# Output gate tiles of a hybrid attention layer: products of 256 moving columns instead of 512

## The chip, the cores and the metric

The kernel runs on one core of a Trainium2 chip. The metric is the device time of one execution, in microseconds (us). The time before is the median of three runs, 2978.56 us.

## What is computed

One decoder layer over 512 tokens of width 2048, in float32. After a norm and a conditioning shift, `h` is projected by `w_in`; one branch is windowed attention, the other a gated delta rule with 32 heads of 128 channels; both are gated, merged and projected back. The part that the change touches is `dz`, the gate of the delta branch's heads:

```
proj = h @ w_in
aq, ak, av, ag, d_qkv, dz, db, da, mg_a, mg_b = split(proj)
...
o = gated_delta_rule(dq, dk, dv, g, beta)
o = rms_norm(o, dn_norm_w) * silu(dz.reshape(B, T, 32, 128))
y_b = o.reshape(B, T, 4096) @ w_o_dn
```

## The kernel before, in words

All large products are made as channel tiles: 128 output channels on the partitions, the 512 tokens as moving columns, one PSUM tile `mm` of 128 x 512. The contraction over 2048 channels goes in 16 steps of 128 (`kt`). Every float32 operand is kept as two reduced-precision parts, `hh` and `hl` for the activations, `whi` and `wlo` for the weights, and a step is three products in `mm3`: `whi` with `hh` (L240), `whi` with `hl` (L241), `wlo` with `hh` (L242). So a tile is 48 products, and each product is recorded with a weight load (PEld) of its own.

Weights come as 1 MB tiles `raw` in a fixed list of jobs (`plan`). They are split in halves of 1024 columns, eight `kt` steps each: ScalarE casts `whi` (L61), VectorE subtracts for `wlo` (L62). Three buffers hold halves. `half` takes the next one, `half_done` frees it and puts the split of a later half and the next load on a list of due work.

The order around the products is set by `pump`. Every second `kt` step, so eight times a tile, `channel_tile` calls it: it starts due splits and loads, and moves each live generator by a step. Generators are the small work of the heads: convolutions, transposes (L274), the products of the scan (L841 to L901), evictions. So passes of other kinds stand between products of a tile. Inside one engine a scheduler then settles the order of what the program issued.

In the stage of the heads (`delta_heads`, `heads`) each of 16 groups makes five tiles: one of queries, two of values, two of gates. The gate tiles are read by `zgate`: ScalarE takes a scaled copy `zh` (L764) and a tanh (L766) from PSUM, VectorE joins them (L768). Two PSUM buffers `mm` take turns.

Names in the rows: `oh` and `ol` are the split activations of a later projection, `po` and `pv` products of the scan, `pto` and `xtp` transposes, `pu`, `py` and `tt` parts of the scan's preparation.

Of the kernel before, what the change touches and what calls it, by code (L numbers as in the profile page):

```python
# [7 lines left out]
F32 = mybir.dt.float32  # L8
# [8 lines left out]
P = 128  # L17
T = 512
D = 2048
KT = D // P  # L20
# [25 lines left out]
class Layer:  # L46
# [197 lines left out]
    def channel_tile(self, name, xh=None, xl=None):  # L244

        xh, xl = (self.hh, self.hl) if xh is None else (xh, xl)
        ps = self.pmm.tile([P, T], F32, tag="mm", name="mm")
        for kt in range(KT):
            if kt % 8 == 0:
                hi, lo = self.half(name)  # L250
            s = slice((kt % 8) * P, (kt % 8) * P + P)
            self.mm3(ps, (hi[:, s], lo[:, s]), (xh[:, kt, :], xl[:, kt, :]), kt == 0, kt == KT - 1)
            if kt % 2:
                self.pump()
            if kt % 8 == 7:
                self.half_done()
        return ps

    def merge_gate(self, name, j, dst):
# [492 lines left out]
    def heads(self, wk, g):  # L752

        st = {"z": []}
        self.go(self.queries(wk, g, self.channel_tile(f"q{g}"), st), 0)
        for e in range(2):
            self.go(self.values(wk, g, e, self.channel_tile(f"v{2 * g + e}"), st), 0)
        for e in range(2):
            self.go(self.zgate(wk, self.channel_tile(f"z{2 * g + e}"), st), 0)

    def zgate(self, wk, ps, st):
        nc = self.nc
# [753 lines left out]
```

## Time and profile before

| | |
|---|---|
| timed runs | 2980.03, 2968.28, 2978.56 us |
| profiled execution | 2967.88 us, span 2966.1 us |
| granted TensorE clock, mean | 0.991 |
| busy: TensorE, weight loads | 2876.7 us, 2355.9 us |
| busy: VectorE, ScalarE, GpSimd | 1775.4, 1089.9, 201.8 us |
| HBM read, written | 415.26 MB, 78.33 MB |

One execution is profiled. Busy time is what an engine's records cover; matmuls overlap, so the start of one product to the start of the next is the pace, not a record's length. A row of the timeline has start, length, engine, line, operation, output and inputs, shapes (weights 128*128, moving 128x512), and in brackets the idle time ahead of it with what ended it. A granted clock of 1.0 is full speed, 0.5 half.

### The profile page before, as it was taken

Reading aid. Unit: us, or ns where it says so; the run is one execution under the profiler, and the core shown is the slowest. Engines: PE = TensorE matmul, PEld = TensorE weight load, DVE = VectorE, ACT = ScalarE, POOL = GpSimd, SP = SyncE. Lnnn points to the kernel's source line nnn. Section 1 sums busy time; section 2 is a strip of 40 time slices with the busy share of each in tenths; the row PEclk is TensorE's granted clock in tenths of the full one; section 3 lists DMA queues with packets and bytes.
Section 4 is the critical chain, followed back from the end, with each engine's and each line's share of the span. In section 5 each row is a group of like instructions: output and inputs, shape, how many; then the busy total and the mean of one; then the engine's idle time right before and its main releaser. Section 6 shows DMA issues by size and latency. Waiting matters only on the chain.

```text
span 2966.1 us, 38006 instructions
## 1 busy us (share of the span) xinstructions
PE 2876.7 (97%) x14524; PEld 2355.9 (79%) x14524; DVE 1775.4 (60%) x2903; ACT 1089.9 (37%) x2103; POOL 201.8 (7%) x188
## 2 busy tenths in 40 slices
PE   6899999999999999999999999999999999999999
PEld 5677777877878778888888888888887887888887
DVE  5766899699865544545454444454545555434666
ACT  3355333333543433333333333333333232222343
POOL 0012220010000000001100000000100000000000
PEclk8999999999999999999999999999999999999999
DMA  9855645632332233333333333334338998855684
GB/s 334 315 161 188 180 134 163 171 96 75 103 116 88 89 132 124 116 122 127 115 124 125 108 122 108 122 115 125 105 114 304 317 320 293 296 169 176 233 325 173
DMA packets 184871, 498.31 MB, mean 168 GB/s; under 512 B 75217, under 2 KB 77777, under 8 KB 147313
## 3 DMA queue, kind: packets, MB, share of 16 engines
q1 hardware_dynamic: 184690, 495.90, 50.1%
q8 instruction: 114, 1.87, 0.3%
q14 instruction: 67, 0.55, 0.1%
HBM read 415.26 MB, written 78.33 MB: 166 GB/s over the span
## 4 chain that ended last, share of the span: by engine, by line
PE 78%; DVE 11%; DMA 6%; ACT 2%; issue 2%; SPq 0%; POOL 0%; DVEq 0%; POOLq 0%; ACTq 0%
PE mm L240 21%; PE mm L241 20%; PE mm L242 20%; DVE wlo L62 2%; PE m L242 2%; PE m L241 2%; PE m L240 2%; DMA oraw<-o_d 2%; DVE A L735 2%; DVE atmp L729 2%; DVE wa L403 1%; DMA E<-g_rows 1%; DMA gw<-in_w_ada_gate 1%; PE po L901 1%; PE pv L882 1%
## 5 line engine op out<-in xcount | busy, mean ns | idle before, releaser
L240 PE MATMUL mm<-hh,whi 128*128 128x512 f32 x2784 | 1134.4, 407 | 3.6 <-ACT mth L263 3.6
L242 PE MATMUL mm<-hh,wlo 128*128 128x512 f32 x2784 | 1093.3, 393 | 0.0
L241 PE MATMUL mm<-hl,whi 128*128 128x512 f32 x2784 | 1091.0, 392 | 0.0
L62 DVE TENSOR_TENSOR wlo<-raw,whi 128x1024 fp32r<-128x1024 f32 (+1 forms) x484 | 590.2, 1221 | 483.7 <-ACT whi L61 460.5
L61 ACT CAST whi<-raw 128x1024 fp32r<-128x1024 f32 (+1 forms) x484 | 504.8, 1044 | 938.6 <-PE mm L241 829.9
L242 PEld LDWEIGHTS mm<-hh,wlo 128*128 128x128 f32 x2784 | 524.8, 189 | 114.2 <-issue 0.7
L240 PEld LDWEIGHTS mm<-hh,whi 128*128 128x128 f32 x2784 | 525.9, 189 | 112.5 <-issue 8.3
L241 PEld LDWEIGHTS mm<-hl,whi 128*128 128x128 f32 x2784 | 526.4, 189 | 99.6 <-issue 0.8
L240 PE MATMUL mm<-oh,whi 128*128 128x512 f32 x512 | 202.5, 397 | 6.9 <-ACT oh L61 6.9
L241 PE MATMUL mm<-ol,whi 128*128 128x512 f32 x512 | 201.6, 394 | 0.6 <-DVE ol L62 0.6
L242 PE MATMUL mm<-oh,wlo 128*128 128x512 f32 x512 | 201.0, 393 | 0.0
L240 PEld LDWEIGHTS mm<-oh,whi 128*128 128x128 f32 x512 | 97.0, 190 | 29.5 <-ACT oh L61 8.6
L241 PEld LDWEIGHTS mm<-ol,whi 128*128 128x128 f32 x512 | 97.2, 190 | 23.0 <-DVE ol L62 2.1
L242 PEld LDWEIGHTS mm<-oh,wlo 128*128 128x128 f32 x512 | 97.3, 190 | 20.4
L735 DVE TENSOR_TENSOR A<-A,atmp 128x62 f32<-128x62 f32 (+30 forms) x124 | 110.8, 894 | 2.0
L729 DVE TENSOR_TENSOR atmp<-A 128x62 f32<-128x62 f32 (+30 forms) x124 | 109.5, 883 | 1.6
L829 POOL TENSOR_TENSOR qe<-qe,yq 128x512 f32<-128x512 f32 x32 | 46.7, 1479 | 921.9 <-DMA qe<-eg_rows 921.9
L698 POOL TENSOR_TENSOR E<-E,neg_g 128x512 f32<-128x512 f32 x64 | 75.0, 1173 | 412.2 <-DMA E<-g_rows 356.9
L875 DVE SCALAR_TENSOR_TENSOR r<-pp,neg_eg,vt 128x128 f32<-128x128 f32 x96 | 29.3, 346 | 92.4 <-PE pp L872 90.5
L1220 ACT ACTIVATE sm<-sm,mx,rs 128x256 f32<-128x256 f32 (+1 forms) x128 | 71.8, 562 | 5.0 <-DVE mx L1215 5.0
L566 DVE SCALAR_TENSOR_TENSOR yv<-mm,convh,yv 128x511 f32<-128x511 f32 (+2 forms) x96 | 71.4, 744 | 1.7
L403 DVE SCALAR_TENSOR_TENSOR wa<-wa,silu_cb 128x2048 f32<-128x2048 f32 x24 | 54.8, 2283 | 6.5 <-DMA silu_cb<-silu_d 6.5
(337 smaller groups left out, 3025.9 us busy)
## 6 DMA issues: line engine op xcount, KB each, us to landing
raw<-in_w_ch SPq DMA_DIRECT2D x158, 1024.0 KB
wa<-in_w_ada_ss SPq DMA_DIRECT2D x32, 1024.0 KB
raw<-in_w_od SPq DMA_DIRECT2D x32, 1024.0 KB
E<-g_rows SPq DMA_DIRECT2D x64, 256.0 KB
q<-in_w_out SPq DMA_DIRECT2D x32, 512.0 KB
gw<-in_w_ada_gate SPq DMA_DIRECT2D x16, 1024.0 KB
f_d<-q SPq DMA_DIRECT2D x32, 512.0 KB
raw<-in_w_os SPq DMA_DIRECT2D x16, 1024.0 KB
```

Source lines behind the costliest of these rows:

```text
L61: self.nc.scalar.copy(out=hi, in_=src)
L62: self.nc.vector.tensor_tensor(out=lo, in0=src, in1=hi.bitcast(F32), op=ALU.subtract)
L240: nc.tensor.matmul(ps, lhsT=wh, rhs=xh, start=first, stop=False)
L241: nc.tensor.matmul(ps, lhsT=wh, rhs=xl, start=False, stop=False)
L242: nc.tensor.matmul(ps, lhsT=wl, rhs=xh, start=False, stop=last)
L403: nc.vector.scalar_tensor_tensor(out=wa, in0=wa, scalar=1.0, in1=scb, op0=ALU.mult, op1=ALU.mult, accum_out=t[:, j : j + 1])
L566: nc.vector.scalar_tensor_tensor(out=y[:, s:], in0=ps[:, : T - s], scalar=w[:, j : j + 1], in1=y[:, s:], op0=ALU.mult, op1=ALU.add)
L698: nc.gpsimd.tensor_tensor(out=E, in0=E, in1=ng, op=ALU.add)
L729: eng.tensor_tensor(out=t, in0=A[:, m : m + 1, m + 1 :].to_broadcast([P, m, n]), in1=A[:, :m, m : m + 1].to_broadcast([P, m, n]), op=ALU.mult,
L735: eng.tensor_tensor(out=A[:, :m, m + 1 :], in0=A[:, :m, m + 1 :], in1=t, op=ALU.add)
L829: nc.gpsimd.tensor_tensor(out=qf, in0=qf, in1=q, op=ALU.mult)
L1220: nc.scalar.activation(t, t, AF.Exp, scale=r[:, h : h + 1], bias=mx[:, h : h + 1], accum_out=den[:, h : h + 1])
```

## The change

The gate tiles are made by a new function, `gate_tile`, in place of `channel_tile`. It takes the same two weight halves in the same order. Within a half it goes over the tokens in two halves of 256, and for each over the eight `kt` steps, so that each weight tile of 128 x 128 is used twice, first for tokens 0 to 255 and then for 256 to 511, in products of 256 moving columns. The start flag stands on the tile's first product alone, the stop flag on its last. `pump` is called after every fourth step of 256 columns, which is eight times a tile as before, and `half_done` after a half's last product.

```diff
+    def gate_tile(self, name):
+
+        ps = self.pmm.tile([P, T], F32, tag="mm", name="mm")
+        for k in range(2):
+            hi, lo = self.half(name)
+            for t in range(2):
+                ts = slice(t * 256, (t + 1) * 256)
+                for j in range(8):
+                    s, kt = slice(j * P, (j + 1) * P), 8 * k + j
+                    x = (self.hh[:, kt, ts], self.hl[:, kt, ts])
+                    self.mm3(ps[:, ts], (hi[:, s], lo[:, s]), x, kt == 0 and t == 0, kt == KT - 1 and t == 1)
+                    if j % 4 == 3:
+                        self.pump()
+            self.half_done()
+        return ps
...
         for e in range(2):
-            self.go(self.zgate(wk, self.channel_tile(f"z{2 * g + e}"), st), 0)
+            self.go(self.zgate(wk, self.gate_tile(f"z{2 * g + e}"), st), 0)
```

On TensorE, the order of the program before, where the last product of a value tile and a pass of the scan (`pqk`) are followed by the first gate tile:

```order
L242 MATMUL mm<-hh,wlo 128x512
L833 MATMUL pqk<-yq,kT 128x128 x4
L240 MATMUL mm<-hh,whi 128x512
L241 MATMUL mm<-hl,whi 128x512
L242 MATMUL mm<-hh,wlo 128x512
```

The same place of the program now:

```order
L242 MATMUL mm<-hh,wlo 128x512
L849 MATMUL pqk<-yq,kT 128x128 x4
L240 MATMUL mm<-hh,whi 128x256
L241 MATMUL mm<-hl,whi 128x256
L242 MATMUL mm<-hh,wlo 128x256
```

From there to the end of the second gate tile 192 products of 256 columns stand where there were 96 of 512. The same passes stand between them: `py` after 24, `pu` after 48, then `ptv`, `pv`, `pd` with `po`, and `pp`.

On VectorE, before, where the first gate tile of a group passes into its second half (`yv` is a convolution of the values, `tt` the solved matrix that the scan takes, `zh` a gate, `vs` an operand of the scan):

```order
L573 SCALAR_TENSOR_TENSOR yv<-th,yv 128x512
L62 TENSOR_TENSOR wlo<-raw,whi 128x1024
L850 TENSOR_TENSOR tt_9047<-pu,neg_beta 64x4x64
L850 TENSOR_TENSOR tt_9049<-pu,neg_beta 64x4x64
L62 TENSOR_TENSOR wlo<-raw,whi 128x1024
L768 SCALAR_TENSOR_TENSOR zh<-zth,zh 128x512
```

The same place now:

```order
L589 SCALAR_TENSOR_TENSOR yv<-th,yv 128x512
L866 TENSOR_TENSOR tt_9047<-pu,neg_beta 64x4x64
L866 TENSOR_TENSOR tt_9049<-pu,neg_beta 64x4x64
L62 TENSOR_TENSOR wlo<-raw,whi 128x1024 x2
L784 SCALAR_TENSOR_TENSOR zh<-zth,zh 128x512
```

One split of a weight half has gone behind the two products into `tt`, once in each of the 16 groups. The orders of ScalarE, GpSimd and the DMA queue are the same as before.

## The prediction

> **What bounds the kernel now.** I first read the page's first section (busy time of each engine, share of the span, instructions) and its chain of work that ended last, then the busy times by stretch for the stage of the heads, where the change lies.
>
> ```profile
> PE 2876.7 (97%) x14524; PEld 2355.9 (79%) x14524; DVE 1775.4 (60%) x2903; ACT 1089.9 (37%) x2103; POOL 201.8 (7%) x188
> PE 78%; DVE 11%; DMA 6%; ACT 2%; issue 2%; SPq 0%; POOL 0%; DVEq 0%; POOLq 0%; ACTq 0%
> 1130.00:2220.00 1090.00, 1090.00 (x5755) 907.14 (x5755) 537.43 (x1007) 403.84 (x897) 94.65 (x91) 1.00 0.36 116
> ```
>
> The columns of the third row are the stretch, its length, then busy time of PE, PEld, DVE, ACT and POOL, granted clock, DMA share and GB/s. TensorE is busy for all 1090 us of the stage at full clock; VectorE has half of it free, ScalarE more. So what the change does to TensorE's time there goes into the end one for one. But busy time is no measure of pace here: records of matmuls overlap. The groups by shape give the length of one product and one weight load:
>
> ```profile
> L240 PE MATMUL mm<-hh,whi 128*128 128x512 f32 x2784 | 1134.4, 407 | 3.6 <-ACT mth L263 3.6
> L241 PEld LDWEIGHTS mm<-hl,whi 128*128 128x128 f32 x2784 | 526.4, 189 | 99.6 <-issue 0.8
> ```
>
> Each of the three products of a step has its own load already, although L240 and L241 use the same weights (2784 loads at L241 too): nothing is shared, and halving the columns doubles the loads. The pace is read from starts. Settled, inside one tile of the heads (timeline of TensorE, first and last of 17 products in a row):
>
> ```profile
> 1403.59 0.39 PE L241 MATMUL mm<-hl,whi 128*128 128x512 f32 x1
> 1407.22 0.39 PE L242 MATMUL mm<-hh,wlo 128*128 128x512 f32 x1
> ```
>
> Sixteen steps in 3.63 us are 0.2269 us a product of 512 columns.
>
> **The change, part by part.** The gate tiles are 32 (16 groups, two each) of 16 x 3 products: 1536 products of 512 columns become 3072 of 256. Now they take 1536 x 0.2269 = 348.5 us of TensorE. The sum hangs on the pace of a 256-column product, and no product of this type with fewer than 512 columns runs in this trace. So I ask what the 0.2269 us are made of, and what the doubled loads need.
>
> *Columns.* There are stretches at half clock. The first and last of ten products in a row there (nine steps), and then three products inside which the clock comes back, each with the row of the next product and the row by stretch that has the clock:
>
> ```profile
> 2464.64 0.63 PE L240 MATMUL mm<-oh,whi 128*128 128x512 f32 x1
> 2468.48 0.63 PE L240 MATMUL mm<-oh,whi 128*128 128x512 f32 x1
> ...
> 2261.12 0.40 PE L241 MATMUL mm<-ol,whi 128*128 128x512 f32 x1
> 2261.36 0.40 PE L242 MATMUL mm<-oh,wlo 128*128 128x512 f32 x1
> 2261.00:2261.30 0.30, 0.30 (x2) 0.20 (x2) 0.09 (x1) 0.00 (x0) 0.00 (x0) 0.77 1.02 375
> ...
> 274.48 0.44 PE L242 MATMUL mm<-hh,wlo 128*128 128x512 f32 x1
> 274.76 0.39 PE L240 MATMUL mm<-hh,whi 128*128 128x512 f32 x1
> 274.50:274.80 0.30, 0.30 (x3) 0.26 (x2) 0.00 (x0) 0.30 (x2) 0.00 (x0) 0.86 0.79 301
> ...
> 629.17 0.58 PE L240 MATMUL mm<-hh,whi 128*128 128x512 f32 x1
> 629.59 0.40 PE L241 MATMUL mm<-hl,whi 128*128 128x512 f32 x1
> 629.40:629.70 0.30, 0.30 (x2) 0.21 (x2) 0.30 (x1) 0.30 (x1) 0.00 (x0) 0.72 0.00 0
> ```
>
> At half clock a product takes 3.84 / 9 = 0.4267 us, that is 1.2 columns a ns and nothing else. At full clock 512 columns at 2.4 a ns would be 0.2133 us; 0.2269 is 13.6 ns more. Either those 13.6 ns are a **cost of each product**, which the change doubles, or the columns come 6% **slower than the clock**, and halves cost nothing. The three products tell: a granted 0.77 over 0.30 us is half clock for 0.138 us, so the clock returned at 2261.138, in the same way at 274.584 and at 629.568. By then 22, 125 and 478 columns were through; the remaining 490, 387 and 34 took 0.222, 0.176 and 0.022 us, which is 18, 15 and 8 ns over their time at 2.4 a ns. A cost of each product would be the same in all three; what comes with columns grows by 456/512 of 13.6 = 12 ns from the last to the first. Measured are 10 ns, with rows rounded to 10 ns. So it leans on columns: 0.2269 / 2 = 0.1135 us a half.
>
> *Loads.* The passes of the scan have 128 columns and a load each, and the load after such a pass shows what a load needs (timelines of TensorE, of weight loads, of TensorE):
>
> ```profile
> 1197.34 0.39 PE L900 MATMUL po<-S,qe 128*128 128x128 f32 x2
> 1198.01 0.39 PE L901 MATMUL po<-vn,E 128*128 128x128 f32 x2
> ...
> 1407.78 0.19 PEld L240 LDWEIGHTS mm<-hh,whi 128*128 128x128 f32 x1
> 1407.89 0.19 PEld L241 LDWEIGHTS mm<-hl,whi 128*128 128x128 f32 x1
> 1408.12 0.19 PEld L242 LDWEIGHTS mm<-hh,wlo 128*128 128x128 f32 x1
> ...
> 1408.12 0.40 PE L241 MATMUL mm<-hl,whi 128*128 128x512 f32 x1
> 1409.05 0.39 PE L242 MATMUL mm<-hh,wlo 128*128 128x512 f32 x1
> ...
> 17.88 8.24 PEld L443 LDWEIGHTS xtp<-dg,xt 128*128 128x128 f32 x70
> ```
>
> Six passes start in 0.67 us: 0.112 each, though a load is recorded with 0.189. Loads follow each other at 0.11 us (1407.78 to 1407.89, two of the very kind in question), and each starts as the product before it starts (1408.12 in both timelines). Seventy loads in a row took (8.24 - 0.19) / 69 = 0.117 each, waits included. So a load fits under a half of 0.1135 us, with 1 or 2 ns to spare where 512 columns left 115. That cover is thin: any slip of load or product now shows in the pace.
>
> *Restarts.* After passes of another kind the products first run slower: from 1408.12 to 1409.05 four steps took 0.93 us, 0.2325 each, 5.6 ns over the settled pace. In the program's order seven such breaks stand ahead of or in the two gate tiles of a group. If some nine products after each lose 4 ns (less than those first four), that is 7 x 36 ns x 16 groups = 4 us, paid today. If the slow stretch is so many products, it stays 4; if it lasts so many us, it holds twice the products and becomes 8.
>
> *Sum.* The bounds are 0.110 us (the loads' closest spacing, the products having no cost of their own) and 0.1135 + 0.0068 = 0.1203 us (all 13.6 ns fixed), plus up to 4 us of restarts: from 3072 x 0.110 - 348.5 = -10.6 us to 3072 x 0.1203 - 348.5 + 4 = +25 us. I take 0.1150, near the value that the three products speak for, with 1.5 ns for the thin cover and the part of the 13.6 ns that they leave open: 353.3 us, **+4.8 us**.
>
> *What moves beside it.* The pumps, which run other work between products, stand at the same points: eight a tile, after the same share of the products; a weight half is released after its last product as before. On VectorE one split per group goes behind two products of the scan:
>
> ```profile
> 1222.00 1.23 DVE L62 TENSOR_TENSOR wlo<-raw,whi 128x1024 fp32r<-128x1024 f32 x1 [0.91 <-ACT whi L61]
> 1223.15 0.74 DVE L850 TENSOR_TENSOR tt<-pu,neg_beta 64x256 f32<-64x256 f32 x2
> ```
>
> VectorE stood idle for 0.91 us before that split, waiting for ScalarE, so the pair of 0.74 us goes largely into the gap, and the split comes at most 0.74 us later. The split is for a half that is used one or two halves on (one is 24 products, 5.4 us), so I cost it at 0; without that cover it would be 16 x 0.74 = 12 us. No instruction moves on ScalarE, GpSimd or the DMA queue, and no wait is added.
>
> The profiled execution took 2967.88 us (span 2966.1): the sum gives 2972.7. The three timed runs have a median of 2978.56, 11 us higher; I add the 4.8 to that: **2983 us**, which is no change: a measurement of this kernel tells about 0.5%, 15 us, from none.
>
> **Rivals.**
> *A cost of each product* (the other side: slower). The feed of each product restarts for 13.6 ns that half clock hides. For it: the excess is constant in the settled rows, and 8 ns remain even with 34 columns left. Against it: the excess shrinks with the columns. Time: 3072 x 0.1203 = 369.6, +21 us, with longer restarts +25: 3000 to 3004. It decides slower from 0.1183 us a half (+15 us).
> *The load shows.* If a load of this type had to end, at its recorded 0.188, before its product, 3072 x 0.188 - 348.5 = +229 us: 3208. Against it stand the 0.112 of the passes and the 0.11 between two loads; for it, that a steady row of such pairs, 192 a group, is not in the trace.
> The Trainium skill, "TensorE: Matmul & The Clock Gate", section "Back-to-back issue gap", speaks for a milder form: in a stream of load and product the spacing is set by both, 81 ns at 128 columns and 131 at 512. A straight line between gives, as an estimate, 98 at 256, so two halves would take 1.5 times one whole, +171 us here; the trace's 227 for 512 shows that these figures aren't this kernel's.
> *The halves run faster.* If the 13.6 ns come from the far end of a long product (a buffer that runs dry), a half takes 256 / 2.4 = 0.1067 us and 3072 x 0.1067 - 348.5 = -21 us, 2958; held by the loads' 0.110 it is -10.6, 2968. For it: the passes of 128 columns start every 0.112 us, where 1.2 columns a ns make 0.107, so they carry little excess. Against: they move half as many columns a ns.
> The same section gives an isolated spacing of N/2.4 + 2.5 ns, 109 at 256 columns, which would be an estimate of -13 us; its 216 for 512 disagrees with the 227 measured.
> *It doesn't do what it says*: the program's order shows 256-column products throughout the gate tiles, so I give this nothing.
>
> **How the numbers follow.** Near columns' pace (0.110 to 0.118): 55%, no change. A cost of each product, alone or with collisions of loads (0.118 to 0.125): 33%, slower. Load showing: 5%, slower. Faster halves: 7%, of which 4 reach beyond 0.5% and 3 stay within. That is faster 0.04, same 0.58, slower 0.38. The range takes in both bounds of the pace: low 2978.6 - 12 = 2966, high 2978.6 + 26 = 3005; the runs of before themselves lie 12 us apart. Left out are the load that shows and most of the faster case.
>
> **What would show it.** In the changed kernel's timeline, starts of 256-column products settle at 0.113 to 0.116 us, each load starting with the product before; 0.120 means the fixed cost, 0.19 the load, 0.107 to 0.110 the faster case. After breaks I expect at most some ns a product more. VectorE's and ScalarE's waits stay as they are, and TensorE is busy throughout the stage. A stage longer by over 15 us, or a wait of TensorE for a split or for VectorE in it, would prove me wrong.

## The result, and the profile after

The changed kernel takes 2986.83 us (median of 11 runs, 2980.56 to 2998.78), the kernel before, run beside it, 2973.35 (11 runs, 2966.49 to 2980.03). The ratio is 1.0048, 95% interval 1.0032 to 1.0064: about 14 us slower, clear of zero, just inside the 0.5% that I had set as the bound of no change, with an interval that reaches beyond it.

The first section of the page after (columns as before):

```profile
span 2983.2 us, 41062 instructions
PE 2891.5 (97%) x16060; PEld 2438.6 (82%) x16060; DVE 1775.0 (59%) x2903; ACT 1089.8 (37%) x2103; POOL 204.3 (7%) x188
```

TensorE has 1536 more products and as many more loads; VectorE and ScalarE have not changed. Where the time is, the first pass of the scan (`pqk`) of the first and of the sixteenth group shows, here in the timeline before:

```profile
1146.44 1.05 PE L833 MATMUL pqk<-yq,kT 128*128 128x128 f32 x8
2156.04 1.05 PE L833 MATMUL pqk<-yq,kT 128*128 128x128 f32 x8
```

and here in the timeline after:

```profile
1150.02 1.05 PE L849 MATMUL pqk<-yq,kT 128*128 128x128 f32 x8
2174.32 1.05 PE L849 MATMUL pqk<-yq,kT 128*128 128x128 f32 x8
```

Fifteen groups take 1009.60 us before and 1024.30 after, 67.307 and 68.287 each. Sixteen times 0.980 is **15.7 us**: the whole change of the two profiled spans (17.1 us) but for 1.4 us. TensorE is still busy without a gap, by stretch:

```profile
1150.02:2174.32 1024.30, 1024.30 (x6781) 919.62 (x6780) 503.50 (x945) 375.24 (x839) 89.01 (x86) 1.00 0.36 116
```

So no new wait came; the products themselves take longer. The first and last of 31 settled products of 256 columns in a row, and two loads beside them:

```profile
1363.48 0.28 PE L240 MATMUL mm<-hh,whi 128*128 128x256 f32 x1
1367.08 0.28 PE L240 MATMUL mm<-hh,whi 128*128 128x256 f32 x1
```

```profile
1363.84 0.19 PEld L241 LDWEIGHTS mm<-hl,whi 128*128 128x128 f32 x1
1363.96 0.19 PEld L242 LDWEIGHTS mm<-hh,wlo 128*128 128x128 f32 x1
```

Thirty steps in 3.60 us are 0.1200 us, not 0.1135. With 256 columns at 2.4 a ns taking 0.1067, that is 13.3 ns over, the same as a product of 512 columns has over its 0.2133. By settled pace a group's gate tiles would grow by 192 x 0.1200 - 96 x 0.2267 = 1.28 us; the group grows by 0.98. Summed over a group's seven stretches of gate products, from the starts in the two timelines, the gate tiles grow by 0.93, so 0.35 is saved at breaks, where a pass of another kind stands between the products; the passes and the tiles behind them take 0.05 more. The net saving is 0.30. One of the seven stretches, from the first `pu` to `ptv`, before (18 products of 512 columns between them):

```profile
1355.66 0.27 PE L847 MATMUL pu<-tt,Y 64*64 64x64 f32 x1
1360.49 0.60 PE L274 MATMUL ptv<-ident,yv 128*128 128x128 f32 x4
```

and after, with 36 of 256 columns:

```profile
1362.41 0.27 PE L863 MATMUL pu<-tt,Y 64*64 64x64 f32 x1
1367.44 0.60 PE L290 MATMUL ptv<-ident,yv 128*128 128x128 f32 x4
```

The stretch grows from 4.83 to 5.03 us, by 0.20, where the settled pace asks for 36 x 0.1200 - 18 x 0.2267 = 0.24. The first, the second and the seventh product of this stretch, in the timeline before and then in the one after:

```profile
1356.27 0.50 PE L240 MATMUL mm<-hh,whi 128*128 128x512 f32 x1
1356.61 0.39 PE L241 MATMUL mm<-hl,whi 128*128 128x512 f32 x1
1357.77 0.39 PE L240 MATMUL mm<-hh,whi 128*128 128x512 f32 x1
...
1363.02 0.39 PE L240 MATMUL mm<-hh,whi 128*128 128x256 f32 x1
1363.24 0.28 PE L241 MATMUL mm<-hl,whi 128*128 128x256 f32 x1
1363.84 0.28 PE L240 MATMUL mm<-hh,whi 128*128 128x256 f32 x1
```

From the first product to the second it is 0.34 and 0.22 us, each some 0.1 over the settled pace. The next five steps take 0.232 each at 512 columns, 5 ns over, and 0.120 at 256, nothing over. So products of 512 columns run slower for a while after a pass of another kind; products of 256 columns do not.

### The profile page after: what moved, and what is told of

Same layout as the page of the kernel before. It is cut to its first block, busy times and chain, and to the rows that moved or that the text cites. A ratio compares the mean times of both kernels' runs of the same rounds, so it can differ in the third digit from the quotient of the medians.

```text
span 2983.2 us, 41062 instructions
## 1 busy us (share of the span) xinstructions
PE 2891.5 (97%) x16060; PEld 2438.6 (82%) x16060; DVE 1775.0 (59%) x2903; ACT 1089.8 (37%) x2103; POOL 204.3 (7%) x188
## 4 chain that ended last, share of the span: by engine, by line
PE 77%; DVE 11%; DMA 7%; issue 2%; ACT 2%; SPq 0%; POOL 0%; DVEq 0%; POOLq 0%; ACTq 0%
PE mm L240 20%; PE mm L241 20%; PE mm L242 20%; DVE wlo L62 2%; DMA oraw<-o_d 2%; DMA gw<-in_w_ada_gate 2%; PE m L240 2%; PE m L242 2%; PE m L241 2%; DVE A L751 2%; DVE atmp L745 2%; DVE wa L419 1%; DMA E<-g_rows 1%; PE po L917 1%; PE pv L898 1%
## 5 line engine op out<-in xcount | busy, mean ns | idle before, releaser
L240 PE MATMUL mm<-hh,whi 128*128 128x512 f32 (+1 forms) x3296 | 1224.3, 371 | 3.6 <-ACT mth L279 3.6
L242 PE MATMUL mm<-hh,wlo 128*128 128x512 f32 (+1 forms) x3296 | 1182.8, 359 | 0.0
L241 PE MATMUL mm<-hl,whi 128*128 128x512 f32 (+1 forms) x3296 | 1181.4, 358 | 0.0
L240 PEld LDWEIGHTS mm<-hh,whi 128*128 128x128 f32 x3296 | 625.9, 190 | 96.6 <-issue 8.3
L242 PEld LDWEIGHTS mm<-hh,wlo 128*128 128x128 f32 x3296 | 625.3, 190 | 93.3 <-issue 0.7
L241 PEld LDWEIGHTS mm<-hl,whi 128*128 128x128 f32 x3296 | 626.5, 190 | 82.2 <-issue 0.8
L240 PE MATMUL mm<-oh,whi 128*128 128x512 f32 x512 | 201.5, 394 | 6.8 <-ACT oh L61 6.8
L241 PE MATMUL mm<-ol,whi 128*128 128x512 f32 x512 | 200.8, 392 | 0.8 <-DVE ol L62 0.6
L240 PEld LDWEIGHTS mm<-oh,whi 128*128 128x128 f32 x512 | 96.5, 189 | 29.5 <-ACT oh L61 8.5
L241 PEld LDWEIGHTS mm<-ol,whi 128*128 128x128 f32 x512 | 96.5, 188 | 24.2 <-DVE ol L62 3.4
L1439 DVE SCALAR_TENSOR_TENSOR gate_bc<-gw,silu_c,gate_bc 128x2048 f32<-128x2048 f32 x15 | 35.3, 2350 | 40.9 <-DMA gw<-in_w_ada_gate 40.9
```

Of the source, the lines that this page charges most:

```text
L240: nc.tensor.matmul(ps, lhsT=wh, rhs=xh, start=first, stop=False)
L241: nc.tensor.matmul(ps, lhsT=wh, rhs=xl, start=False, stop=False)
L242: nc.tensor.matmul(ps, lhsT=wl, rhs=xh, start=False, stop=last)
L1439: nc.vector.scalar_tensor_tensor(out=acc, in0=w, scalar=s, in1=acc, op0=ALU.mult, op1=ALU.add)
```

## The experiments

Two theories stood at first. **P**: each product costs 13.3 ns beside its columns, at full clock. **L**: columns come 6% slower than the clock, as I had predicted, and 0.120 us is what a load of 128 weights with its handover needs.

**Other tiles, hardly any breaks.** The gate tiles go back to 512 columns, and the 32 tiles of the delta branch's output projection are made by the new function:

```diff
-            self.go(self.zgate(wk, self.gate_tile(f"z{2 * g + e}"), st), 0)
+            self.go(self.zgate(wk, self.channel_tile(f"z{2 * g + e}"), st), 0)
...
-                    ps = self.channel_tile(f"od{half}_{j}", oh, ol)
+                    ps = self.gate_tile(f"od{half}_{j}", oh, ol)
```

> Gate tiles are back at 512 columns; the 32 tiles of the delta branch's output projection, in which hardly any pass of another kind stands, are made in 256-column products instead. Theory P (each product costs 13.3 ns beside its columns at full clock): starts 0.120 us apart, nothing saved at breaks, so 1536 x 13.3 ns = +20 us on the kernel before, less what the other order of steps saves of the waits at the two starts of that stage. At half clock a 256-column product takes 0.2133 us, the cost hidden. Theory L (columns come at 0.4427 ns each, and 0.120 is the pace of a load of 128 columns with its handover): also 0.120 and about +20 us; at half clock also 0.213. Theory S (the +14 of the change is all there is to such tiles, the seven breaks a group save nothing): +14 us.

Measured: 2991.07 us against 2972.05, ratio 1.0068, interval 1.0044 to 1.0092, that is +20 us (13 to 27). Its timeline, the first and last of 100 products in a row, and of ten at half clock:

```profile
2299.88 0.28 PE L241 MATMUL mm<-ol,whi 128*128 128x256 f32 x1
2311.76 0.28 PE L241 MATMUL mm<-ol,whi 128*128 128x256 f32 x1
...
2258.29 0.41 PE L240 MATMUL mm<-oh,whi 128*128 128x256 f32 x1
2260.21 0.41 PE L240 MATMUL mm<-oh,whi 128*128 128x256 f32 x1
```

11.88 / 99 = 0.1200 us at full clock, 1.92 / 9 = 0.2133 at half, where nothing is over. That is +20 as P and L said; theory S's +14 lies within the interval too, so the time alone doesn't exclude it. What the rows of the heads show, a saving at breaks, agrees: where breaks are few, the full price is paid.

**Other widths.** The tokens in parts of 384 and 128 columns, and of 320 and 192:

```diff
-                ts = slice(t * 256, (t + 1) * 256)
+                ts = slice(t * 384, 384 + t * 128)
```

```diff
-                ts = slice(t * 256, (t + 1) * 256)
+                ts = slice(t * 320, 320 + t * 192)
```

> Gate tiles with the tokens in parts of 384 and 128 columns. Theory P (13.3 ns a product): 384 columns start 0.1733 us apart; 128 columns would be 0.0667, so their loads bound them, at 0.108 to 0.112 as the scan's passes; in all 1536 x (0.1733 + 0.110) - 348 = +87 us. Theory L (columns at 0.4427 ns, loads at 0.120): 384 columns 0.1700 us apart, 128 columns 0.120, +97 us.

> Gate tiles with the tokens in parts of 320 and 192 columns. Theory P (13.3 ns a product): 320 columns start 0.1467 us apart, 192 columns would be 0.0933 and are held by their loads at 0.108 to 0.112; 1536 x (0.1467 + 0.110) - 348 = +46 us. Theory L (columns at 0.4427 ns, loads at 0.120): 0.1417 and 0.120, +54 us.

Measured: 3064.03 and 3014.07 us, one run each, +92 and +42 on 2972.05. Timeline of the first, 18 steps of 384 columns and 21 of 128:

```profile
1231.26 0.33 PE L241 MATMUL mm<-hl,whi 128*128 128x384 f32 x1
1234.38 0.33 PE L241 MATMUL mm<-hl,whi 128*128 128x384 f32 x1
...
1235.60 0.28 PE L241 MATMUL mm<-hl,whi 128*128 128x128 f32 x1
1237.94 0.27 PE L241 MATMUL mm<-hl,whi 128*128 128x128 f32 x1
```

Timeline of the second, 18 steps of 320 columns and 21 of 192:

```profile
1234.75 0.31 PE L242 MATMUL mm<-hh,wlo 128*128 128x320 f32 x1
1237.39 0.31 PE L242 MATMUL mm<-hh,wlo 128*128 128x320 f32 x1
...
1238.08 0.27 PE L241 MATMUL mm<-hl,whi 128*128 128x192 f32 x1
1240.42 0.28 PE L241 MATMUL mm<-hl,whi 128*128 128x192 f32 x1
```

3.12 / 18 = 0.1733 and 2.64 / 18 = 0.1467 us: both are the columns at 2.4 a ns plus 13.3 ns, to the last digit that P gave. L's 0.1700 and 0.1417 fall. (The two times alone decide less: +42 is nearer to P's +46, +92 lies between P's +87 and L's +97.) Products of 128 and 192 columns take the same 2.34 / 21 = 0.111 us on average, so columns don't set the pace there. The load of 128 weights that each of them has is the likely bound, at 0.111 and not at L's 0.120; no run has so few columns with a shorter load. As an estimate, such a bound would show below some 234 columns, (0.111 - 0.0133) us at 2.4 a ns. So L is out on both counts, and a load fits under a half as predicted.

**Shorter loads.** Is it the product that costs, or the load that runs beside it? In the second weight half, loads of 64 channels in place of 128 (all into the first 64 output channels):

```diff
+            m = 64 if k else P
+            for t in range(4 if k else 1):
+                ts = slice((t % 2) * 256, (t % 2 + 1) * 256) if k else slice(0, T)
...
+                    s, kt = slice(j * P + (t // 2) * 64, j * P + (t // 2) * 64 + m), 8 * k + j
...
+                    self.mm3(ps[0:m, ts], (hi[:, s], lo[:, s]), x, j + t == 0, j == 7 and t == 3 * k)
```

> In the gate tiles the second weight half is used in loads of 64 channels (all into the first 64 output channels, overwriting what the first half left there, so the gates are not the reference's): 96 products of 256 columns a tile with loads half as long; the first half stays at 24 products of 512. Theory P (13.3 ns a product, whatever the load): 256-column products start 0.120 us apart; 32 x (24 x 0.2267 + 96 x 0.120) - 348 = +195 us. Theory L (0.120 is the pace of a load of 128 columns): with loads of 64 the columns bound, 0.1133 us apart, +174 us.

Measured: 3160.24 us, one run, +188, between the two. The timeline has both paces, 39 steps after one pass and 36 after another:

```profile
1182.12 0.28 PE L241 MATMUL mm<-hl,whi 128*64 128x256 f32 x1
1186.54 0.28 PE L241 MATMUL mm<-hl,whi 128*64 128x256 f32 x1
...
1187.32 0.28 PE L241 MATMUL mm<-hl,whi 128*64 128x256 f32 x1
1191.64 0.28 PE L241 MATMUL mm<-hl,whi 128*64 128x256 f32 x1
```

4.42 / 39 = 0.1133 and 4.32 / 36 = 0.1200 us. The same product with the same load settles at 6.7 ns over its columns or at 13.3, by what came before it: in all 16 groups 0.1133 after the passes `pu`, `ptv` and `po`, 0.1200 after `pp`. P in its strict form, a cost that nothing but the product sets, is wrong. I formed theory **C**: the load takes the time from the columns that flow beside it, in proportion to its weights.

**Shorter loads still.** The second weight half in 48 products of 512 columns with loads of 64, then 96 of 256 columns with loads of 32:

```diff
+            parts = [(64, 0, 0, T), (64, 64, 0, T), (32, 0, 0, 256), (32, 32, 0, 256), (32, 64, 256, T), (32, 96, 256, T)]
+            for m, c, t0, t1 in parts if k else [(P, 0, 0, T)]:
...
```

> In the gate tiles the first weight half is used as in the kernel before (24 products of 512 columns, loads of 128 channels); the second in 48 products of 512 columns with loads of 64 channels and then 96 of 256 columns with loads of 32, all into the first 64 or 32 output channels, each part overwriting the one before, so the gates are not the reference's. Theory C (each load takes time from the columns that flow beside it: 16 steps of 0.833 ns for 128 weights, half for 64, a quarter for 32): settled starts 0.2200 us apart at 512 columns with loads of 64, and 0.1100 at 256 with loads of 32. Theory P (a cost of each product, 13.3 ns whatever is loaded): 0.2267 and 0.1200. The kernel before has no such products; against its 348 us for the gate tiles C gives 32 x (24 x 0.2267 + 48 x 0.220 + 96 x 0.110) - 348 = +502 us, P +543.

Measured: 3499.89 us, one run, +528. Timeline, 18 steps with loads of 64 and 51 with loads of 32:

```profile
1291.19 0.40 PE L241 MATMUL mm<-hl,whi 128*64 128x512 f32 x1
1295.33 0.40 PE L241 MATMUL mm<-hl,whi 128*64 128x512 f32 x1
...
1204.01 0.28 PE L241 MATMUL mm<-hl,whi 128*32 128x256 f32 x1
1209.79 0.28 PE L241 MATMUL mm<-hl,whi 128*32 128x256 f32 x1
```

4.14 / 18 = 0.2300 and 5.78 / 51 = 0.1133 us. C's 0.2200 and 0.1100 fail, P's 0.2267 and 0.1200 too. With 32 weights it is 6.7 ns in this stretch, while behind `ptv` and `pv` single steps wander between 0.112 and 0.120; with 64 under 512 columns single steps keep wandering, and the mean of these 18 is 16.7 ns over.

**Addresses.** The kernel before, with the weights of the channel tiles stored 8, and in another run 2, elements apart (here for 2):

```diff
-            s = slice((kt % 8) * P, (kt % 8) * P + P)
+            s = (kt % 8) // 2 * 256 + kt % 2
+            s = slice(s, s + 255, 2)
...
-    ch = lambda w: w.reshape(KT, P, -1, P).transpose(2, 1, 0, 3).reshape(-1, P, KT * P)
+    ch = lambda w: w.reshape(KT // 2, 2, P, -1, P).transpose(3, 2, 0, 4, 1).reshape(-1, P, KT * P)
```

> The kernel before, all tiles at 512 columns, with the weights of the channel tiles stored so that the 128 columns of one load stand 8 elements apart (eight kt steps interleaved). Theory C with collisions that hang on addresses (load and columns meet at the same place of the memory): the 13.3 ns of a product become something else, between 0 and some 100 ns, so starts at 0.2133 to 0.32 us instead of 0.2267; with 9888 such products 1 ns is 10 us of the kernel. Theory C without addresses, and theory P: 0.2267 and the time of the kernel before, within 0.3%.

> The kernel before, all tiles at 512 columns, with the weights of the channel tiles stored so that the 128 columns of one load stand 2 elements apart (pairs of kt steps interleaved): the load then goes through its addresses as fast as the moving columns do (0.833 ns for two elements). Theory C with collisions that hang on addresses: the two meet once at most instead of again and again, starts at 0.2133 to 0.216 us, up to 9888 x 13 ns = -130 us; or they meet always and it is far slower. Theory C without addresses, and theory P: 0.2267, the time of the kernel before within 0.3%.

Measured: with 8 apart 3131.14 us, ratio 1.0539 (1.0521 to 1.0557); with 2 apart 3004.18, ratio 1.0110 (1.0089 to 1.0130), both against 2971.77. The loads by shape with 8 apart:

```profile
L241 PEld LDWEIGHTS mm<-hl,whi 128*128 128x128 f32 x2784 | 920.5, 331 | 1.1 <-issue 0.2
```

They are recorded with 331 ns instead of 189, and the weight loads hardly stand idle (1.1 us ahead of those of L241, where it was 99.6). The loads may well be the bound here: 142 ns on the 0.111 us of a contiguous load makes, as an estimate, 0.253 us, and 44 products in a row (from 2424.81 us) start 0.245 apart. So this run can't tell what happens beside the columns. With 2 apart, by shape, and 42 settled steps of 512 columns in the timeline:

```profile
L241 PEld LDWEIGHTS mm<-hl,whi 128*128 128x128 f32 x2784 | 541.1, 194 | 95.4 <-issue 0.8
```

```profile
2300.11 0.39 PE L240 MATMUL mm<-oh,whi 128*128 128x512 f32 x1
2309.91 0.39 PE L240 MATMUL mm<-oh,whi 128*128 128x512 f32 x1
```

The loads are 5 ns longer and far from the bound, yet a product takes 9.80 / 42 = 0.2333 us, 20 ns over its columns. So what a product costs hangs on how its weights lie.

**Both together.** The changed kernel with weights 2 apart; beside the edit above, in the gate tiles:

```diff
-                    s, kt = slice(j * P, (j + 1) * P), 8 * k + j
+                    s, kt = slice(j // 2 * 256 + j % 2, j // 2 * 256 + 256, 2), 8 * k + j
```

> The changed kernel (gate tiles in 256 columns) with the weights of all channel tiles stored 2 elements apart. Theory C (the cost of a product comes from its load running beside the columns, and hangs on the load's addresses): 256-column products settle 6.7 ns slower, at 0.1267 us, as the 512-column ones did (0.2333 for 0.2267). Theory P (a cost of the product itself, which the 512-column products then show for another reason): 0.120 at 256 columns. In both the 512-column products stay at 0.2333; against the run with the same weights and gate tiles of 512 columns that is, less some 5 us saved after breaks, C: 3072 x 0.1267 - 1536 x 0.2333 - 5 = +26 us, P: +5 us.

Measured: 3014.24 us, one run, 10 us over the one with weights 2 apart and gate tiles of 512, nearer to P's +5 than to C's +26. Timeline, 27 steps of 256 columns and 6 of 512:

```profile
1380.07 0.28 PE L240 MATMUL mm<-hh,whi 128*128 128x256 f32 x1
1383.31 0.28 PE L240 MATMUL mm<-hh,whi 128*128 128x256 f32 x1
...
1395.44 0.39 PE L241 MATMUL mm<-hl,whi 128*128 128x512 f32 x1
1396.84 0.39 PE L241 MATMUL mm<-hl,whi 128*128 128x512 f32 x1
```

0.1200 and 0.2333 us. C's 0.1267 fails; the half keeps its 13.3 ns while the whole has 20. What sets the 6.7, 13.3 or 20 ns stays open: the load takes part in it, but not as a sum over its weights. What is settled is what the change turned on: with the weights as this kernel lays them, products of 256, 320, 384 and 512 columns, each with a load of 128 weights, cost 13.3 ns each beside their columns. No run pointed to a version faster than the kernel before.

## Why the prediction went as it did

The forecast was +4.8 us and 2983 us, the measurement about +14 and 2986.83, inside the range. A clear loss is what the first rival said, not the forecast. By my own signs I was wrong: the starts settled at 0.120 us, and the stage grew by 15.7 us, over the 15 that I had named. The two times also look closer than the two changes are: 2983 stands on a time before of 2978.56, and beside the change the kernel before took 2973.35.

*What bounds the kernel*: right. TensorE's time in the heads went into the end one for one, 15.7 us of the span's 17.1.

*Columns*: this step failed. I read three products inside which the clock came back, saw their excess shrink with the columns left, and concluded that the 13.6 ns come with the columns (0.1135 us a half). The widths of 256, 320 and 384 show the same 13.3 ns each: it is a cost of each product, my first rival, at the 0.120 us that it gave. A product in which the clock changes was no stand-in for a settled one: right behind a return of the clock or a pass of another kind, single products of 512 columns start 0.22 to 0.24 us apart (timeline before, from 1356.61), a scatter as large as the 10 ns that I read, from rows rounded to 10 ns. Why the excess shrinks with the columns left isn't settled. The term was 3072 x 0.1150 - 348.5 = +4.8; with the measured pace it is 3072 x 0.1200 - 348.5 = +20.1.

*Loads*: right. Each load starts with the product before (in the changed kernel at 1363.84 both a product of L240 and the load for L241) and fits under a half: products of 128 and 192 columns, loads included, go at 0.111 us. The rival in which the load shows did not come. The 0.112 of the scan's passes was weaker evidence than I took it for, since 128 columns at 1.2 a ns, the pace that my third rival gave those passes, already make 0.107.

*Restarts*: wrong in sign. I said that 4 us were paid and would stay or double. The size was near (the slow steps of a group before add up to some 0.22 us, 3.5 us in 16 groups), but the 512-column products alone paid it: halves show no slow stretch, and net of the 0.05 us that a group's other work lost, 16 x 0.30 = 4.8 us came back. That is why the kernel lost 14 to 16 us and not the 21 to 25 of the rival. The two errors, +15.3 and -4.8, are of opposite sign. That the sum came within some 10 us of the measurement is luck in part: the pace that it rests on was wrong.

*What moves beside it*: right as far as the profile shows. VectorE's and ScalarE's busy times agree within 0.4 us, and TensorE has no gap in the stage.

The Trainium skill's isolated spacing of N/2.4 + 2.5 ns for N columns ("TensorE: Matmul & The Clock Gate", section "Back-to-back issue gap") has the right form, a fixed cost beside the columns; the size for this operand type is 13.3 ns in these runs.

## What to carry to other kernels

When an operation's shape changes, the question is which part of its pace is fixed and which goes with its size; one run at a third size settles it, while a transient in a trace may point the wrong way. Here each product paid a fixed 13.3 ns beside its columns, 213 ns of them at full width, and halving the columns doubled how often it was paid. Below some width products went no faster than 0.111 us each, so in a kernel like this one, where each product has its own load, products should be as wide as they may be. Slow stretches after a change of work are worth measuring apart, since they may go the other way.

## What the runs showed of the hardware

- Settled at full clock, a product of the reduced-precision type with a load of 128 weights takes its columns at 2.4 a ns plus 13.3 ns: 0.1200 us at 256, 0.1467 at 320, 0.1733 at 384, 0.2267 at 512. At half clock it takes its columns at 1.2 a ns and nothing beside: 0.2133 at 256.
- At 128 and at 192 columns such products go at the same 0.111 us.
- The surplus is not one number: at 256 columns with loads of 32 or 64 weights 6.7 ns after some passes and more after others, 20 ns at 512 columns with weights 2 elements apart.
- A load whose weights stand 8 elements apart is recorded with 331 ns instead of 189, and the kernel is 5.4% slower.
- After a pass of another kind, products of 512 columns run slower for a while (0.232 us in the five steps shown, against 0.2267); products of 256 columns don't (0.120).
